# A hybrid attention layer on one core: a weight split sooner, a root's steps on another engine, and more banks for turns

## The chip, the core and the metric

The kernel runs on one core of a Trainium2 chip. Its engines are TensorE (PE, with PEld for its weight loads), VectorE (DVE), ScalarE (ACT), GpSimd (POOL) and SyncE (SP, which only issues transfers). The metric is the device time of one execution in microseconds; the time before is the median of three runs.

## The reference

One decoder layer over 2048 tokens of width 1024. The input is normalised and modulated, and one projection feeds two mixers: forgetting attention over 8 heads (causal, with a cumulative log gate) and sliding-window attention over 8 query heads with 2 key/value heads, window 128 and sinks. Each result is multiplied by a SiLU gate path, both are joined, projected, normalised and added to the input.

```python
mod = jax.nn.silu(c) @ w_ada[l] + b_ada[l]
shift, scale, gate = jnp.split(mod, 3, axis=-1)
h = rms_norm(x, g_pre[l]) * (1.0 + scale[:, None, :]) + shift[:, None, :]
proj = h @ w_in[l]
qa, ka, va, fa, za, qb, kb, vb, zb = jnp.split(proj, split_points, axis=-1)
oa = forgetting_attention(..., fa + b_fgate[l]) * jax.nn.silu(za)
ob = sliding_window_sink_attention(rope(qb), rope(kb), vb, sinks[l]) * jax.nn.silu(zb)
y = jnp.concatenate([oa, ob], axis=-1) @ w_out[l]
x = x + gate[:, None, :] * rms_norm(y, g_post[l])
```

## The kernel before

**Numbers and shapes.** Each float32 operand is held as two float16 parts, high and low, and each product is three matmuls: high by high, high by low, low by high. The tokens are taken in four groups of 512 (`ci`, 0 to 3). The normalised, modulated input of a group is `hT[ci]`, transposed: 8 tiles `k` of 128 features by 512 tokens, each with a high and a low part.

**From x to hT.** For each group, `load_x` brings four tiles `xt` of 128 tokens; `squares` (L404, ScalarE) sums their squares; `root` takes the reciprocal root by an integer seed (L100, L105, L106), a halving (L107) and three Newton steps (L114, L115, L117), all on VectorE; `normal` (L416, VectorE; L414, ScalarE, in group 0) scales the tiles. `turn(ci, k)` transposes one feature tile on TensorE into one of five banks of the pool `ps_x` (L422); its `scaled` applies the factors `Gp` and `Shp` on ScalarE (L428: one pass for even `k` to the high part, and one to `hf`; for odd `k` only `hf`), and its `split` makes the high part of odd `k` (L432) and all low parts (L433) on VectorE.

**The opening.** The modulation is computed from `w_ada`; then a maximum over the bound of h goes through two tiny matmuls (L641, L644) and gives `Gp` and `Shp`. Turns 0 to 4 of group 0 are done before that, the last three follow as banks come free, and the steps of `root(1)` are threaded between the splits of group 0.

**Weights.** A 128-column block of the input weights is a key: kb, vb, zb0 to zb3, qb0 to qb3, va, qk, za. Each is loaded (`w_load`, GpSimd's queue, L216, 512 KB), its maximum taken on VectorE (`w_max`, L222) and sent to memory and back to all partitions (`w_back`, L225 and L230), turned into a scale (`w_scale`), and split into a high part on ScalarE (`w_high`, L256) and a low one on VectorE (`w_low`, L262).

**The order.** All unit lists are concatenated by `add` into `punits`. A unit is the work of one `k` for kb, zb and qb (three matmuls, L339), or of half a token tile for vb (twelve, L777); eight units make one chunk of 512 tokens, after which the bank is evacuated in steps that `after` puts a number of ticks later. `events` holds the small steps by the number of the unit in front of which they are issued: `at_slice` adds one, and `add` sets a key's preparation by its lead ahead of the key's first unit. Within a region each engine issues in the order written. A group of tokens is kb, vb, zb0 (24 units), and the 8 turns of the next group are strewn among them after the units in `at_` (32 entries a group); group 3 has kb and vb alone. Then come qb0, zb0, qb0, zb1 up to unit `N_PRO` = 144. From there on 32 windows of the sliding-window attention (`Pair`: scores, maxima, exps, turn, pv) share TensorE with the remaining units up to `N_SWA`, spread evenly: 296 units. Forgetting attention and the output projection follow.

The rotary step of kb and qb chunks (`evac_rope`) copies the projection (L731), swaps halves by four transfers `qs` on SP's queue (L733), multiplies by the cosine (L736) and sine (L746), and adds (L747). `spread` brings the tables for a group.

Of the kernel before, what the change touches and what calls it, by code (L numbers as in the profile page):

```python
# [10 lines left out]
F32 = mybir.dt.float32  # L11
# [8 lines left out]
P = 128  # L20
# [23 lines left out]
def hybrid_layer(  # L44
# [46 lines left out]

    def rsqrt_mean(dst, ss, n):

        for _ in rsqrt_parts(dst, ss, n):
            pass

    def rsqrt_parts(dst, ss, n, more=None):
        v = sm(n, "rs_v")
        if more is None:
            V.tensor_scalar(v[:], ss, 1.0 / D, EPS, op0=ALU.mult, op1=ALU.add)  # L100
        else:
            V.scalar_tensor_tensor(v[:], ss, 1.0 / D, more, op0=ALU.mult, op1=ALU.add)
        y = sm(n, "rs_y")
        h = small.tile([P, n], I32, tag="rs_h", name="rs_h")
        V.tensor_scalar(h[:], v[:].bitcast(I32), 1, None, op0=ALU.logical_shift_right)  # L105
        V.tensor_scalar(y[:].bitcast(I32), h[:], -1, 0x5F3759DF, op0=ALU.mult, op1=ALU.add)  # L106
        V.tensor_scalar(v[:], v[:], -0.5, None, op0=ALU.mult)  # L107
        for it in range(3):
            yield
            t = sm(n, "rs_t")  # L110
            if n == 1:
                V.scalar_tensor_tensor(t[:], y[:], y[:], v[:], op0=ALU.mult, op1=ALU.mult)
            else:
                V.tensor_tensor(t[:], y[:], y[:], op=ALU.mult)  # L114
                V.tensor_tensor(t[:], t[:], v[:], op=ALU.mult)  # L115
            y2 = dst if it == 2 else sm(n, "rs_y")
            V.scalar_tensor_tensor(y2[:], t[:], 1.5, y[:], op0=ALU.add, op1=ALU.mult)  # L117
            y = y2
# [287 lines left out]
    def root(ci):  # L406
        ss, rst = rstd[ci]
        rsqrt_mean(rst, ss[:], 4)

# [7 lines left out]

    def turn(ci, k):

        px = ps_x.tile([P, CH], F32, tag="x", name="px")  # L420
        for u in range(4):
            PE.transpose(px[:, u * P:(u + 1) * P], xt[ci * 4 + u][:, k * P:(k + 1) * P], ident[:])  # L422
        hf = hst.tile([P, CH], F32, tag="hf", name="hf")
        hi, lo = hT[ci][:, 0, k, :], hT[ci][:, 1, k, :]

        def scaled():
            for dst in ([hi] if k % 2 == 0 else []) + [hf[:]]:
                A.activation(dst, px[:], AF.Identity, scale=Gp[:, k:k + 1], bias=Shp[:, k:k + 1])  # L428

        def split():  # L430
            if k % 2:
                V.tensor_copy(hi, hf[:])  # L432
            V.tensor_tensor(lo, hf[:], hi, op=ALU.subtract)  # L433

        return scaled, split
# [17 lines left out]
    with tc.manual_schedule():  # L453
# [186 lines left out]

        PE.transpose(bk[0][0:1, 0:P], bmx[:], ident[:])  # L641
        bm = st.tile([1, 1], F32, name="bm")
        V.tensor_reduce(bm[:], bk[0][0:1, 0:P], axis=AX.X, op=ALU.max)
# [6 lines left out]

        V.tensor_scalar(pfl[:], ipH[:], 0.5, None, op0=ALU.mult)
        root1 = rsqrt_parts(rstd[1][1], rstd[1][0][:], 4)
        for k in range(KT):
            turned[k][0]()
            turned[k][1]()
            if k >= 2:
                next(root1, None)
            if k + 5 < KT:
                turned.append(turn(0, k + 5))
        V.tensor_reduce(mxs[:, 2:3], wq["zb0"][0][:], axis=AX.XY, op=ALU.max, apply_absolute_value=True)  # L660
# [279 lines left out]
    def add(key, us):  # L940
        if key not in pkeys and key not in ("kb", "vb"):
            at = len(punits) - {"za3": 4}.get(key, 20 if key[:2] == "za" else 0)
            for n, (lead, f) in enumerate(((42, lambda: w_load(key, pieces(key))), (31, lambda: w_max(key)),
# [3 lines left out]
                if n >= 4 and key[:2] in ("qk", "za"):  # L947
                    lead -= 1
                if n < 4 and key in ("qb0", "zb1"):
                    lead += (16, 14, 12, 4)[n]  # L950
                if key == "zb0":
                    if n >= 3:
                        events.setdefault((13, 13, 14, 15, 16)[n - 3], []).append(f)
                else:
                    events.setdefault(max(at - lead, n), []).append(f)
# [30 lines left out]
    for ci in range(NCH):  # L986
# [3 lines left out]
        if ci < 3:  # L990
            add(*others[ci])

            mine, punits[n0:] = punits[n0:], []
            at_ = ([14, 16, 17, 18, 19, 20, 21, 22], [6, 8, 10, 12, 14, 16, 18, 20], [6, 7, 9, 10, 12, 13, 15, 16])[ci]
            for n, u in enumerate(mine):
# [3 lines left out]
            if ci < 2:  # L999

                for u in range(4):
                    at_slice(n0 + (3 if ci else 9) + u, lambda ci=ci, u=u: squares(ci + 2, (u,)))
                    at_slice(len(punits) - (0 if ci else 10) + u, lambda ci=ci, u=u: normal(ci + 2, (u,)))
                at_slice(len(punits) - 13, lambda ci=ci: root(ci + 2))
            at_slice(n0 + 12, lambda ci=ci: spread(ci + 1))
# [5 lines left out]
    add("qb0", qb_units(0, 1))  # L1011
    add(*others[4])
    N_PRO = len(punits)
    for n in range(4):
        at_slice(N_PRO + 20 + 3 * n, lambda: next(fx["sums"], None))
    qbs = [(f"qb{c_ // 4}", qb_units(c_ // 4, c_ % 4)) for c_ in range(2, 16)]
    n_o = 5
    for n, (key, us) in enumerate(qbs):
        add(key, us)
        lim = 5 + 5 * (n + 1) // 4 if n + 1 < len(qbs) else len(others)  # L1020
        for key2, us2 in others[n_o:lim]:
            add(key2, us2)
        n_o = lim
# [705 lines left out]
```

## Time and profile before

| What | Value |
|---|---|
| Median of three runs | 1177.23 us (1176.5 to 1177.47) |
| Profiled execution, its own time | 1173.47 us |
| Its span | 1171.7 us |
| TensorE busy | 1126.7 us (96%) |
| VectorE busy | 924.3 us (79%) |
| ScalarE busy | 661.7 us (56%) |
| GpSimd busy | 182.4 us (16%) |
| Chain that ended last, by engine | PE 74%, DVE 13%, DMA 7%, ACT 3%, issue 2% |

Busy time is the union of an engine's instructions. TensorE's includes matmuls stretched by a lower granted clock. The chain is followed back from the last instruction, at each step to what released it. In a timeline row the columns are start, duration, engine, line, operation and tiles, and in brackets the idle time before it with what ended that.

### The profile page before, as it was taken

The page shows a single profiled execution, that of the slowest core. Times are in us where ns is not written, and L with a number is a line of the kernel's source. Part 1 is how long each engine was busy: PE and PEld are TensorE (multiplying, and loading weights), DVE is VectorE, ACT ScalarE, POOL GpSimd, SP SyncE. Part 2 cuts the span into 40 slices and gives each one's busy share as a digit, 9 for nine tenths or more (in the row PEclk, how much of TensorE's full clock was granted, in tenths as well). Part 3 has the DMA queues.
Part 4 walks back from the last instruction along what each step waited for, and adds up shares of the span by engine and source line. Part 5 has one row for each costly group of instructions (what it writes and reads, how often), then busy time and mean ns, then how long its engine had stood idle before and what let it go on. Part 6 is the DMA issues. An engine that isn't in the chain of part 4 may idle for free.

```text
span 1171.7 us, 26770 instructions
## 1 busy us (share of the span) xinstructions
PE 1126.7 (96%) x10637; PEld 671.1 (57%) x10637; DVE 924.3 (79%) x2167; ACT 661.7 (56%) x1150; POOL 182.4 (16%) x293
## 2 busy tenths in 40 slices
PE   5899999999999999999999999999999999999997
PEld 2476555765558876555555555555556555544444
DVE  7876668677776548788888999888897897778885
ACT  2784445454555421476666767666676788633332
POOL 1000125535454421010000100001000000000000
PEclk9899999999999999999999999999999999999999
DMA  9745333314324323423424332222311237677742
GB/s 333 259 142 88 82 94 78 91 52 108 95 70 95 48 60 74 67 56 86 74 71 65 106 55 58 61 49 67 52 37 43 72 88 226 138 216 200 193 144 108
DMA packets 123481, 120.19 MB, mean 103 GB/s; under 512 B 64948, under 2 KB 100828, under 8 KB 123356
## 3 DMA queue, kind: packets, MB, share of 16 engines
q1 hardware_dynamic: 112088, 85.69, 27.1%
q0 software_dynamic: 10832, 32.50, 13.0%
q8 instruction: 83, 1.36, 0.6%
q14 instruction: 42, 0.34, 0.2%
q10 hardware_dynamic: 436, 0.28, 0.1%
HBM read 64.75 MB, written 25.18 MB: 77 GB/s over the span
## 4 chain that ended last, share of the span: by engine, by line
PE 74%; DVE 13%; DMA 7%; ACT 3%; issue 2%; SPq 1%; POOL 0%; DVEq 0%; ACTq 0%; POOLq 0%
PE bk L339 27%; PE bk L1522 13%; PE bk L357 7%; PE sta L1311 4%; PE sta L1310 4%; PE bk L1261 4%; PE poa L1336 3%; PE poa L1337 3%; PE poa L1334 3%; DMA wa<-in_w_ada_dram 2%; DVE a_m L1264 2%; PE pss L871 1%; PE pob L924 1%; DVE pha L1324 1%; PE pxb L900 1%
## 5 line engine op out<-in xcount | busy, mean ns | idle before, releaser
L1317 ACT ACTIVATE p<-sta,lift,scl_qk 128x1024 f32<-128x1024 f32 (+2 forms) x160 | 171.9, 1075 | 131.1 <-PE sta L1311 80.4
L339 PE MATMUL bk<-hT,wh_qk 128*128 128x512 f16 x768 | 194.7, 378 | 0.0
L1324 DVE TENSOR_TENSOR pha<-p,pha 128x1024 f16<-128x1024 f32 (+2 forms) x160 | 169.1, 1057 | 0.2 <-ACT pha L1321 0.2
L1264 DVE TENSOR_REDUCE a_m<-bk 128x1 f32<-128x512 f32 x192 | 130.4, 686 | 46.5 <-PE bk L1261 45.5
L1522 PE MATMUL bk<-wohl,oz 128*128 128x512 f16 x744 | 165.3, 379 | 1.0 <-DVE oz L1471 0.7
L1321 ACT ACTIVATE pha<-p 128x1024 f16<-128x1024 f32 (+2 forms) x160 | 148.1, 925 | 7.1 <-PE bk L1261 2.3
L1522 PEld LDWEIGHTS <-oz 128*128 128x128 f16 x744 | 71.9, 99 | 82.8 <-DVE oz L1471 1.8
L1337 PE MATMUL poa<-vt,pha 128*128 128x65 f16 x1088 | 116.0, 192 | 1.4 <-DVE pha L1324 1.4
L1334 PE MATMUL poa<-vt,pha 128*128 128x65 f16 x1088 | 116.6, 193 | 0.8 <-DVE ona L1343 0.7
L1336 PE MATMUL poa<-vt,pha 128*128 128x64 f16 x1088 | 116.6, 194 | 0.0
L339 PEld LDWEIGHTS <-wh_qk 128*128 128x128 f16 x768 | 72.2, 97 | 74.4 <-issue 1.9
L1310 PE MATMUL sta<-T 128*128 128x512 f16 (+1 forms) x320 | 110.9, 346 | 2.8 <-ACT p L1317 2.8
L1261 PE MATMUL bk<-T 66*128 66x512 f16 (+2 forms) x320 | 109.7, 348 | 2.5 <-DVE a_m L1264 1.9
L1334 PEld LDWEIGHTS <-pha 128*128 128x128 f16 x1088 | 101.5, 96 | 15.5 <-DVE ona L1343 1.9
L1311 PE MATMUL sta<-T 69*128 69x512 f16 (+1 forms) x320 | 109.8, 348 | 0.0
L1336 PEld LDWEIGHTS <-pha 128*128 128x128 f16 x1088 | 100.9, 97 | 11.4
L1337 PEld LDWEIGHTS <-pha 128*128 128x128 f16 x1088 | 100.8, 99 | 1.8 <-DVE pha L1324 1.8
L339 PE MATMUL bk<-hT,wh_za 128*128 128x512 f16 x384 | 99.7, 378 | 0.0
L357 PE MATMUL bk<-wh_va,hT 128*128 128x128 f16 x1536 | 91.9, 221 | 2.9 <-issue 2.8
L357 PEld LDWEIGHTS <-hT 128*128 128x128 f16 x1536 | 88.7, 99 | 7.4 <-issue 5.4
L339 PE MATMUL bk<-hT,wh_zb 128*128 128x512 f16 x384 | 88.9, 379 | 0.0
L339 PE MATMUL bk<-hT,wh_qb 128*128 128x512 f16 x384 | 87.6, 379 | 0.7 <-DVE wh_qb L262 0.7
(447 smaller groups left out, 1893.1 us busy)
## 6 DMA issues: line engine op xcount, KB each, us to landing
hT<-in_x_dram SPq DMA_DIRECT2D x20, 512.0 KB
wa<-in_w_ada_dram SPq DMA_DIRECT2D x16, 512.0 KB
z_d<-tz POOLq DMA_DIRECT2D x32, 256.0 KB
T<-stq SPq DMA_DIRECT2D x64, 128.0 KB
T<-z_d SPq DMA_DIRECT2D x16, 512.0 KB
out_dram<-hT SPq DMA_DIRECT2D x15, 512.0 KB
xt<-in_x_dram SPq DMA_DIRECT2D x12, 512.0 KB
qs<-qf SPq DMA_DIRECT2D x80, 64.0 KB
```

What stands on the lines that cost most here:

```text
L339: PE.matmul(ps, whl[:, a, k, :], hT[ci][:, b, k, :], start=(k == 0 and n == 0), stop=(k == KT - 1 and n == 2))
L357: PE.matmul(ps[:, u * P:(u + 1) * P], hT[ci][:, a, k, u * P:(u + 1) * P], whl[:, b, k, :], start=(k == 0 and n == 0), stop=(k == KT - 1 an ...
L1261: PE.matmul(mx[:, :w], T[0:XM, 0, i * P:(i + 1) * P], T[0:XM, 2, pc * CH:pc * CH + w], start=True, stop=True)
L1264: V.tensor_reduce(m3[:, u, pc:pc + 1], mx[:, :w], axis=AX.X, op=ALU.max)
L1310: PE.matmul(self.st[:, o:o + w], T[:, 3, kb_], T[:, 1, qc], start=True, stop=False)
L1311: PE.matmul(self.st[:, o:o + w], T[0:XR, 2, kb_], T[0:XR, 0, qc], start=False, stop=not diag)
L1317: A.activation(self.p32[:, :self.w], self.st[:, :self.w], AF.Exp, scale=scl[f"qk{self.hd}"][:], bias=lift[:])
L1324: V.tensor_tensor(self.ph[:, 1, :self.w], self.p32[:, :self.w], self.ph[:, 0, :self.w], op=ALU.subtract)
L1334: PE.matmul(po[:, u, :], ph[:, 0, pq], vt[:, b, hd, 0:65], start=(self.first and n == 0 and u == 0), stop=False)
L1336: PE.matmul(po[:, u, 0:64], ph[:, 0, pq], vt[:, b, hd, 65:VW], start=False, stop=False)
L1337: PE.matmul(po[:, u, :], ph[:, 1, pq], vt[:, b, hd, 0:65], start=False, stop=(self.last and n == len(self.blocks) - 1))
L1522: PE.matmul(py, self.hl[:, i, k, :], w_slot(8 * j + k)[:, cc], start=(k == 0 and m_ == 0), stop=(k == KT - 1 and m_ == 2))
```

## The change

1. `root(ci)` for the groups 1 to 3 does the halving and the Newton steps on GpSimd; the seed stays on VectorE. GpSimd takes two operations where VectorE has one fused, so a root has 13 operations there.
2. Turns 5 and 6 of group 0 go into the banks `bk[1]` and `bk[2]`, issued between the two tiny matmuls; turn 7 is issued behind the scaling of turn 0. `root(1)` is issued as a whole ahead of the scalings.
3. zb1 is loaded at unit 6, its maximum taken at 38, sent back at 46, scaled at 67, split at 71 to 75. Its chunks 0 and 1 become units of the third token group (ci = 2), which then has 40 units, and chunk 2 takes the place that chunk 0 had. `N_PRO` becomes 160, and the windows hold 280 units.
4. The turns of group 3 are strewn after the units 14, 16, ... 28 of that group instead of 6, 7, ... 16.
5. Places of the small steps: `root(2)` at unit 14 instead of 19; `squares(3)` at 56 to 59 instead of 35 to 38; `root(3)` at 61 instead of 51; `normal(3)` at 68 to 71 instead of 64 to 67.
6. In the windows, the order of the other keys' chunks is adapted: one of zb1's chunks is left for the first three qb chunks.

```diff
@@ -89,12 +89,13 @@
         V.tensor_scalar(t[:], src, 1.0e-30, None, op0=ALU.max)
         V.tensor_scalar(dst.bitcast(I32), t[:].bitcast(I32), 0x7F800000, None, op0=ALU.bitwise_and)
 
-    def rsqrt_mean(dst, ss, n):
-
-        for _ in rsqrt_parts(dst, ss, n):
+    def rsqrt_mean(dst, ss, n, eng=None):
+
+        for _ in rsqrt_parts(dst, ss, n, eng=eng):
             pass
 
-    def rsqrt_parts(dst, ss, n, more=None):
+    def rsqrt_parts(dst, ss, n, more=None, eng=None):
+        W = eng or V
         v = sm(n, "rs_v")
         if more is None:
             V.tensor_scalar(v[:], ss, 1.0 / D, EPS, op0=ALU.mult, op1=ALU.add)
@@ -104,17 +105,21 @@
         h = small.tile([P, n], I32, tag="rs_h", name="rs_h")
         V.tensor_scalar(h[:], v[:].bitcast(I32), 1, None, op0=ALU.logical_shift_right)
         V.tensor_scalar(y[:].bitcast(I32), h[:], -1, 0x5F3759DF, op0=ALU.mult, op1=ALU.add)
-        V.tensor_scalar(v[:], v[:], -0.5, None, op0=ALU.mult)
+        W.tensor_scalar(v[:], v[:], -0.5, None, op0=ALU.mult)
         for it in range(3):
             yield
             t = sm(n, "rs_t")
             if n == 1:
-                V.scalar_tensor_tensor(t[:], y[:], y[:], v[:], op0=ALU.mult, op1=ALU.mult)
+                W.scalar_tensor_tensor(t[:], y[:], y[:], v[:], op0=ALU.mult, op1=ALU.mult)
             else:
-                V.tensor_tensor(t[:], y[:], y[:], op=ALU.mult)
-                V.tensor_tensor(t[:], t[:], v[:], op=ALU.mult)
+                W.tensor_tensor(t[:], y[:], y[:], op=ALU.mult)
+                W.tensor_tensor(t[:], t[:], v[:], op=ALU.mult)
             y2 = dst if it == 2 else sm(n, "rs_y")
-            V.scalar_tensor_tensor(y2[:], t[:], 1.5, y[:], op0=ALU.add, op1=ALU.mult)
+            if eng is None:
+                V.scalar_tensor_tensor(y2[:], t[:], 1.5, y[:], op0=ALU.add, op1=ALU.mult)
+            else:
+                W.tensor_scalar(t[:], t[:], 1.5, None, op0=ALU.add)
+                W.tensor_tensor(y2[:], t[:], y[:], op=ALU.mult)
             y = y2
 
     def root_scale(dst, ss):
@@ -405,7 +410,7 @@
 
     def root(ci):
         ss, rst = rstd[ci]
-        rsqrt_mean(rst, ss[:], 4)
+        rsqrt_mean(rst, ss[:], 4, G if ci else None)
 
     def normal(ci, us=range(4)):
         for u in us:
@@ -415,9 +420,9 @@
             else:
                 V.tensor_scalar(xt[t], xt[t], r, None, op0=ALU.mult)
 
-    def turn(ci, k):
-
-        px = ps_x.tile([P, CH], F32, tag="x", name="px")
+    def turn(ci, k, px=None):
+
+        px = px or ps_x.tile([P, CH], F32, tag="x", name="px")
         for u in range(4):
             PE.transpose(px[:, u * P:(u + 1) * P], xt[ci * 4 + u][:, k * P:(k + 1) * P], ident[:])
         hf = hst.tile([P, CH], F32, tag="hf", name="hf")
@@ -639,6 +644,7 @@
         V.tensor_reduce(bmx[:], bnd[:], axis=AX.X, op=ALU.max)
 
         PE.transpose(bk[0][0:1, 0:P], bmx[:], ident[:])
+        turned += [turn(0, k, bk[k - 4]) for k in (5, 6)]
         bm = st.tile([1, 1], F32, name="bm")
         V.tensor_reduce(bm[:], bk[0][0:1, 0:P], axis=AX.X, op=ALU.max)
         PE.matmul(bk[0][:, P:P + 1], ones[0:1, :], bm[:], start=True, stop=True)
@@ -649,14 +655,12 @@
         V.tensor_scalar(Shp[:], shf[:], ipH[:], 2.0 ** 14, op0=ALU.mult, op1=ALU.mult)
 
         V.tensor_scalar(pfl[:], ipH[:], 0.5, None, op0=ALU.mult)
-        root1 = rsqrt_parts(rstd[1][1], rstd[1][0][:], 4)
+        root(1)
         for k in range(KT):
             turned[k][0]()
             turned[k][1]()
-            if k >= 2:
-                next(root1, None)
-            if k + 5 < KT:
-                turned.append(turn(0, k + 5))
+            if k == 0:
+                turned.append(turn(0, 7))
         V.tensor_reduce(mxs[:, 2:3], wq["zb0"][0][:], axis=AX.XY, op=ALU.max, apply_absolute_value=True)
         for key in ("kb", "vb"):
             kaps[key] = kappa(pws[key], key)
@@ -946,8 +950,10 @@
                                            (5, lambda: w_low(key, 1)), (4, lambda: w_done(key)))):
                 if n >= 4 and key[:2] in ("qk", "za"):
                     lead -= 1
-                if n < 4 and key in ("qb0", "zb1"):
+                if n < 4 and key == "qb0":
                     lead += (16, 14, 12, 4)[n]
+                if key == "zb1":
+                    lead = at - (6, 38, 46, 67, 71, 73, 75, 77)[n]
                 if key == "zb0":
                     if n >= 3:
                         events.setdefault((13, 13, 14, 15, 16)[n - 3], []).append(f)
@@ -989,9 +995,12 @@
         add("vb", vb_units(ci))
         if ci < 3:
             add(*others[ci])
+            if ci == 2:
+                add(*others[4])
+                add(*others[5])
 
             mine, punits[n0:] = punits[n0:], []
-            at_ = ([14, 16, 17, 18, 19, 20, 21, 22], [6, 8, 10, 12, 14, 16, 18, 20], [6, 7, 9, 10, 12, 13, 15, 16])[ci]
+            at_ = ([14, 16, 17, 18, 19, 20, 21, 22], [6, 8, 10, 12, 14, 16, 18, 20], [14, 16, 18, 20, 22, 24, 26, 28])[ci]
             for n, u in enumerate(mine):
                 punits.append(u)
                 if n in at_:
@@ -999,9 +1008,9 @@
             if ci < 2:
 
                 for u in range(4):
-                    at_slice(n0 + (3 if ci else 9) + u, lambda ci=ci, u=u: squares(ci + 2, (u,)))
-                    at_slice(len(punits) - (0 if ci else 10) + u, lambda ci=ci, u=u: normal(ci + 2, (u,)))
-                at_slice(len(punits) - 13, lambda ci=ci: root(ci + 2))
+                    at_slice(n0 + (24 if ci else 9) + u, lambda ci=ci, u=u: squares(ci + 2, (u,)))
+                    at_slice(len(punits) + (4 if ci else -10) + u, lambda ci=ci, u=u: normal(ci + 2, (u,)))
+                at_slice(len(punits) - (3 if ci else 18), lambda ci=ci: root(ci + 2))
             at_slice(n0 + 12, lambda ci=ci: spread(ci + 1))
     n0 = len(punits)
     at_slice(n0, lambda: open_fox())
@@ -1009,15 +1018,15 @@
     add("qb0", qb_units(0, 0))
     add(*others[3])
     add("qb0", qb_units(0, 1))
-    add(*others[4])
+    add(*others[6])
     N_PRO = len(punits)
     for n in range(4):
         at_slice(N_PRO + 20 + 3 * n, lambda: next(fx["sums"], None))
     qbs = [(f"qb{c_ // 4}", qb_units(c_ // 4, c_ % 4)) for c_ in range(2, 16)]
-    n_o = 5
+    n_o = 7
     for n, (key, us) in enumerate(qbs):
         add(key, us)
-        lim = 5 + 5 * (n + 1) // 4 if n + 1 < len(qbs) else len(others)
+        lim = (7, 8, 8)[n] if n < 3 else 5 + 5 * (n + 1) // 4 if n + 1 < len(qbs) else len(others)
         for key2, us2 in others[n_o:lim]:
             add(key2, us2)
         n_o = lim
```

## The prediction

> **What bounds the kernel now.** I read the page first (span and busy lines), then the busy time of each engine in stretches through the opening projections, then the timelines of TensorE, ScalarE, VectorE and the queues there, and last the waits of the sliding-window stage.
>
> ```profile
> span 1171.7 us, 26770 instructions
> ## 1 busy us (share of the span) xinstructions
> PE 1126.7 (96%) x10637; PEld 671.1 (57%) x10637; DVE 924.3 (79%) x2167; ACT 661.7 (56%) x1150; POOL 182.4 (16%) x293
> ```
>
> TensorE is the bound, 96% busy. The change adds and removes no matmul, so it can only move the end by the time that TensorE loses in the stretch that it reorders. That stretch, cut at the borders of its unit groups (columns as in the first line, each engine's busy time with its instructions):
>
> ```profile
> core 0: us, PE busy (x) PEld busy (x) DVE busy (x) ACT busy (x) POOL busy (x), PEclk, DMA share, GB/s
> 46.14:56.32 10.18, 8.84 (x36) 4.60 (x36) 8.93 (x26) 7.32 (x11) 0.00 (x0) 0.83 0.45 144
> 56.32:72.42 16.10, 15.32 (x157) 12.10 (x156) 14.43 (x46) 12.07 (x22) 0.00 (x0) 1.00 0.66 221
> 72.42:79.61 7.19, 6.09 (x29) 2.80 (x28) 6.85 (x13) 6.00 (x9) 0.00 (x0) 1.00 0.31 74
> 79.61:93.55 13.94, 13.94 (x150) 11.15 (x149) 8.13 (x27) 10.66 (x21) 1.47 (x2) 1.00 0.44 110
> 98.25:117.68 19.43, 17.18 (x156) 12.92 (x157) 10.07 (x18) 7.73 (x14) 2.56 (x4) 0.91 0.68 87
> 117.68:129.88 12.20, 11.18 (x121) 8.02 (x120) 10.69 (x29) 5.29 (x9) 1.09 (x2) 1.00 0.48 102
> ```
>
> "Busy" also counts matmuls drawn out by a slow clock, so I set the stretches against clean rates. The chain that ended last has undisturbed runs of both matmul shapes:
>
> ```profile
> 124.37 5.68 PE bk L777 x96
> ...
> 158.50 5.93 PE bk L339 x27
> ```
>
> 96 vb matmuls take 5.68 us (0.71 a unit of 12), and one 512-wide matmul 0.22 (0.66 a unit of 3, 5.27 for 24). The stretch from 79.61 to 93.55 has no idle time: 5.68 + 5.27 leaves 2.99 for its seven turns, 0.43 each. Then the third group's stretch (one kb unit, 8 vb, 8 zb0, 8 turns) should take 0.66 + 5.68 + 5.27 + 3.44 = 15.05 and takes 19.43: 4.4 lost. The fourth group's kb and vb should take 10.95 and take 12.20: 1.25 lost. The first kb chunk with three turns should take 6.56 and takes 10.18: 3.6 lost. The two stretches from 56.32 to 79.61 lose 1.2 and 1.5, with 0.5 allowed for the small matmuls of the zb0 maximum. So about 12 us are there to be won, 1% of the span.
>
> **The change part by part.**
>
> *Turns into two more banks, the first root's Newton steps off VectorE.* TensorE:
>
> ```profile
> 43.86 0.38 PE L644 MATMUL bk<-bm,ones 1*128 1x1 f32 x2 [0.37 <-DVE bm L643]
> ```
>
> The eight transposes of turns 5 and 6 now stand just ahead of L644: 0.87 us from about 43.4, so L644 starts near 44.3, and Gp, on which all scaling waits, is 0.45 late. That is a cost on the path. ScalarE behind it:
>
> ```profile
> 45.31 0.78 ACT L428 ACTIVATE hT<-px,Shp,Gp 128x512 f16<-128x512 f32 x1 [2.76 <-DVE pfl L651]
> ...
> 51.96 1.50 ACT L428 ACTIVATE hf<-px,Shp,Gp 128x512 f32<-128x512 f32 x2
> ```
>
> It needs the same 8.1 us for its 12 scalings (45.31 to 53.46) and ends at 53.9. VectorE ended its splits here:
>
> ```profile
> 55.15 0.69 DVE L433 TENSOR_TENSOR hT<-hf,hT 128x512 f16<-128x512 f32 x1
> ```
>
> A cast and a subtraction, about 1.0 us, have to follow the last scaling: 54.9 instead of 55.84, because ten small Newton operations left this loop, which had drawn it 1.4 us past what ScalarE's end requires. The seed's three operations come before the loop, while VectorE waits for the first scaling anyway. Gain 0.9. This root's result is wanted only by a normalisation some 10 us later.
>
> *The second root, and what the transfers allow (to the end of the second kb chunk).*
>
> ```profile
> 65.21 0.16 DVE L100 TENSOR_SCALAR rs_v<-ss 128x4 f32<-128x4 f32 x1
> ...
> 67.40 0.16 DVE L117 SCALAR_TENSOR_TENSOR rst<-rs_t,rs_y 128x4 f32<-128x4 f32 x1
> 67.80 0.69 DVE L746 TENSOR_TENSOR qs<-qs,sinT 128x512 f32<-128x512 f32 x1 [0.24 <-DMA qs<-qf]
> ...
> 70.74 1.41 DVE L416 TENSOR_SCALAR xt<-xt,rst 128x1024 f32<-128x1024 f32 x2
> ...
> 78.38 0.69 DVE L433 TENSOR_TENSOR hT<-hf,hT 128x512 f16<-128x512 f32 x1
> ```
>
> 13 operations run from 65.21 to 67.56, 0.18 each; ten leave, 1.8 us, ahead of the splits that hold up the second kb chunk until 79.07. With the 0.9 that would be 2.7. But L746 was waiting for its transfer qs, so qs decides what is kept, and qs is queued behind the loads of x:
>
> ```profile
> 50.41 4.84 SPq L397 DMA_DIRECT2D xt<-in_x_dram  x8
> ```
>
> The loads wait for the last turn of group 0, which now needs only the first turn's bank: two scalings from 45.8 end at 47.1, the turn at 47.6, 2.8 sooner than 50.4. Against that zb1's 512 KB join them. I allow 1.3 us, from the 403 GB/s of this stretch:
>
> ```profile
> 30.00:40.00 10.00, 9.54 (x16) 4.12 (x17) 7.65 (x21) 9.07 (x12) 0.00 (x0) 0.69 1.02 403
> ```
>
> qs comes 1.5 sooner. I take **1.5** (bounds 0 and 2.7) by the end of the second kb chunk.
>
> *The third root, its squares, and the third group.* VectorE, and TensorE's wait for it:
>
> ```profile
> 85.23 0.69 DVE L433 TENSOR_TENSOR hT<-hf,hT 128x512 f16<-128x512 f32 x1 [5.23 <-ACT hf L428]
> ```
>
> ```profile
> PE px L422 <- DVE xt L416: 2.3, 4, 0.9
> ```
>
> ```profile
> 97.60:101.10 3.50, 1.60 (x6) 0.51 (x4) 3.50 (x6) 0.00 (x0) 0.56 (x1) 1.00 0.43 100
> 101.10:104.50 3.40, 3.05 (x14) 2.18 (x15) 2.47 (x4) 2.34 (x4) 1.45 (x2) 0.50 0.23 82
> 104.50:108.00 3.50, 3.50 (x55) 3.48 (x53) 1.63 (x4) 2.13 (x4) 0.00 (x0) 1.00 1.45 40
> ```
>
> The squares of the last token group stood on ScalarE ahead of the third group's scalings and left VectorE idle 5.23 us; VectorE then reached the last normalisations far behind TensorE, whose turns waited 2.3 us for them, and after 3.5 us with 1.60 busy the granted clock was 0.50 for 3.4 us. That makes up the 4.4. Now these squares go behind the third group's turns, and the fourth's turns start eight units later in their group. Does the normalisation make it?
>
> ```profile
> L404 ACT ACTIVATE junk<-xt x8: 1047/1056/1059, 57.0 to 82.7; 128x1024 bf16<-128x1024 f32 x8
> L404 ACT ACTIVATION_READ_ACCUMULATOR junk<-xt x8: 185/187/201, 58.0 to 83.7; 128x1 f32 x8
> ```
>
> Before the squares' place (unit 56) TensorE has 8 vb, 2 zb0 and 5 turns from 79.61 on, 9.15 us: 87.3 with the 1.5. Four squares (5.0) and one turn's scalings (1.3) end at 93.6, the seed at 94.2. TensorE reaches the turn at 98.25 - 1.5 + 0.66 + 7 x 0.71 = 102.4, and four normalisations take 2.7. So GpSimd has 5.5 us for 13 operations, 0.42 each. No row shows such operations on it; the nearest are these:
>
> ```profile
> L910 POOL TENSOR_SCALAR_AFFINE_SELECT ptb<-fold 128x512 f16<-128x512 f16 x64 | 40.7, 636 | 54.2 <-ACT fold L905 51.3 <-DVE fold L906 2.7
> ...
> L1713 POOL MEMSET const-float32-0.0<- 128x1 f32 x1 | 0.1, 99 | 0.3 <-issue 0.3
> ```
>
> 0.10 to 0.64 each; four elements are nearest to the memset of one, and each step waits for the one before: I take 0.25, 3.3 us for a root. That fits by 2.2 us here, and by 1.0 at the second root, where 4.3 pass between the seed's end (64.9) and the first normalisation (69.2 for 70.74). So the 4.4 return whole.
>
> The page "TensorE: Matmul & The Clock Gate" of the Trainium skill (Part 1) says that the clock halves after a whole idle window of about 3.4 us. By that rule none of these waits would have cost clock, the 2.1 us beyond the 2.3 of waiting would stay lost, and the forecast would be 1174.2. The trace disagrees: the longest of the four waits was 0.9 us, and the clock fell. I keep the rows.
>
> *Two chunks of zb1 in the third group.* 16 units, 10.5 us of TensorE work, move ahead of the fourth kb chunk. Its splits have that much longer, so the 1.25 lost there return. zb1's load goes past GpSimd's z_d store and qb0's load; its maximum and split on VectorE come where that engine idled. Behind its round trip through memory GpSimd holds a z_d store, qb0's load and, 15 units on, the third root; none is wanted within 7 us. For small stalls around the moved pieces (bounds 0 and 2.3, one more wait like L416's) I charge 0.8.
>
> *The sliding-window stage gives them up.* Its 32 windows held 296 units, now 280: 0.33 us less cover in each.
>
> ```profile
> ACT fold L905 <- PE pxb L900: 31.5, 25, 3.8
> ```
>
> In 25 of them ScalarE waited for TensorE's transposes, so that cover isn't missed. In seven it may be: at most 2.3. I take 1.2.
>
> **Sum.** 1.5 + 4.4 + 1.25 - 0.8 - 1.2 = 5.15 us sooner. The profiled execution took 1173.47 (1.8 beside the span): 1168.3. The median of the runs is 3.8 higher, 1177.23, and I keep that distance: **1172.1**.
>
> **The rivals.**
> - *Newton on GpSimd is slow, and it ends slower.* At 0.64 us an operation a root takes 8.3. The second root holds VectorE's normalisation up 4.0, the third the turns 2.8, and that gap halves the clock again, about 2: 5.15 - 8.8 = 3.65 slower, 1180.9. It crosses zero near 0.50 an operation. For it: GpSimd's long row is 0.64. Against: that row has 128 times the elements. The page "GPSIMD Engine Reference" of the Trainium skill (section 4.1) advises VectorE for elementwise work, GpSimd being about twice as slow with two inputs; no run here shows it yet. By it, an estimate of 0.36 us from VectorE's 0.18, a root takes 4.7 and is 0.4 late once: 1172.5.
> - *zb1's load runs badly beside x.* Between 104.50 and 108.00, above, the DMA engines were full at only 40 GB/s. Should that happen for 8 us from 48 on, x and qs come 5.2 late, the squares and the zb0 split behind them hold TensorE, and the gap halves the clock: 5.15 - 1.5 - 5.2 - 2 = 3.55 slower, 1180.8. Against it: one such stretch, and an empty queue before the x loads into which zb1 may slip.
> - *The windows give it all back.* If each window is as long as its chain of scores, maxima and exponentials, 10.5 us are lost: 4.15 slower, 1181.4. The 25 waits speak against it.
>
> **How the numbers follow.** Forecast 0.65, with an own range of 1168.9 (2.7 + 4.4 + 1.25 kept, nothing lost) to 1174.7 (half of it spoilt); slow GpSimd 0.13, bad load 0.12, windows 0.10. 0.2% is 2.4 us, about what can be told from no change. The rivals act by degrees: a fifth of their 0.35 still ends faster, two fifths the same. Faster 0.72, same 0.14, slower 0.14. The range is 1168.5 to 1178.5; only the rivals at their full prices lie outside.
>
> **What would show it.** No TensorE wait for L416 at the fourth group's turns, and a full clock there; the last squares behind the third group's turns on ScalarE; GpSimd's 13 operations a root at about 0.25 us; the x loads near 47.6; the first L746 near 66.3; no new TensorE waits in the windows. I am wrong if GpSimd's operations exceed 0.42, if zb1's load delays x, or if TensorE idles over 2 us more in the windows.

## The result, and the profile after

Medians: 1175.43 us after (14 runs, 1172.07 to 1180.7), 1176.55 before (14 runs, 1173.54 to 1179.46); ratio 0.9993, 95% interval 0.9979 to 1.0006. That is no change that this measurement can tell; 1.1 us sooner at best guess, where 5.15 was forecast. The profiled execution after took 1175.42 us.

```profile
span 1173.7 us, 26784 instructions
...
PE 1129.2 (96%) x10637; PEld 671.6 (57%) x10637; DVE 920.0 (78%) x2137; ACT 661.1 (56%) x1150; POOL 196.6 (17%) x332
```

Busy time of the engines of the changed kernel, in stretches cut at the borders that the prediction used: both kb chunks to the end of the second; the second group's rest; the third group, which now holds 16 units more; the fourth group's kb and vb.

```profile
core 0: us, PE busy (x) PEld busy (x) DVE busy (x) ACT busy (x) POOL busy (x), PEclk, DMA share, GB/s
46.22:77.88 31.66, 29.27 (x212) 18.26 (x212) 27.51 (x60) 25.37 (x41) 9.12 (x24) 0.95 0.57 176
77.88:91.81 13.93, 13.93 (x150) 11.15 (x149) 8.72 (x19) 7.76 (x16) 1.70 (x3) 1.00 0.34 82
91.81:126.29 34.48, 32.01 (x226) 20.38 (x225) 22.86 (x48) 19.52 (x34) 7.22 (x19) 0.95 0.40 92
126.29:137.15 10.86, 10.86 (x122) 8.03 (x121) 4.84 (x17) 2.76 (x5) 1.44 (x2) 1.00 0.38 104
```

Before, the same stretches took 33.47, 13.94, 24.13 and 12.20 (from its borders 46.14, 79.61, 93.55, 117.68, 129.88). With 10.54 for the 16 moved units (5.27 for eight, as in the prediction), the third group takes 23.94: 0.2 of its 4.4 has come back. The first stretch gained 1.8 and the fourth 1.3. From there to the end of the span it is 1036.55 after, and 1041.82 - 10.54 = 1031.28 before: 5.3 later. The profiled execution before lies 3.1 us below the median of its kernel (1173.47 against 1176.55), the one after at its median, so part of these 5.3 can be the difference between two executions.

The third group first, in the timeline of the changed kernel (start, duration, engine and line, and in brackets the idle time before it and what ended that):

```profile
79.39 2.47 SPq L737 DMA_DIRECT2D qs<-qf  x4
79.69 0.54 POOL L230 DMA_DIRECT2D mx_d<-w_mx  x1 [0.50 <-DVE w_mx L227]
...
88.62 0.54 POOL L235 DMA_DIRECT2D mxr<-mx_d  x1 [8.39 <-DMA mx_d<-w_mx]
...
89.09 0.69 DVE L750 TENSOR_TENSOR qs<-qs,sinT 128x512 f32<-128x512 f32 x1 [4.18 <-DMA cosT<-cs__234]
...
90.54 0.63 ACT L754 ACTIVATE stb<-qc 128x512 f16<-128x512 f32 x1 [3.95 <-DVE qc L751]
...
97.64 0.17 DVE L101 TENSOR_SCALAR rs_v<-ss 128x4 f32<-128x4 f32 x1 [1.53 <-ACT junk L409]
...
98.78 0.38 PE L344 MATMUL bk<-hT,wh_kb 128*128 128x512 f16 x1 [2.03 <-DVE hT L437]
```

The four qs transfers were issued by 81.9, and VectorE could use them at 89.1. (The bracket of L750 names cosT because its signal came last; that transfer stands behind qs on the same queue and brings a table for the next group, which L750 does not read.) ScalarE, which issues in order, stood 3.95 us before `stb`, its float16 copy of the rotated chunk. The moved squares behind it came that much later: the third root's seed, forecast at 94.2, started at 97.64. The last scalings and splits stood behind the squares, and TensorE waited. Its granted clock then fell to 0.52 (in the columns of the stretches above). On the chain that ended last the 84 vb matmuls behind that wait take 6.60 us, where the rate of the 96 in 5.68 gives 4.97.

```profile
100.50:103.90 3.40, 3.40 (x35) 3.40 (x33) 1.92 (x6) 1.63 (x2) 2.64 (x9) 0.52 0.03 11
```

```profile
100.10 6.60 PE bk L781 x84
```

Then the first windows, in the columns of a timeline:

```profile
153.25 0.54 POOL L230 DMA_DIRECT2D mx_d<-w_mx  x1 [3.29 <-DVE w_mx L227]
153.51 2.41 SPq L737 DMA_DIRECT2D qs<-qf  x4
...
167.88 0.69 DVE L750 TENSOR_TENSOR qs<-qs,sinT 128x512 f32<-128x512 f32 x1 [6.25 <-DMA qs<-qf]
...
169.33 0.63 ACT L754 ACTIVATE stb<-qc 128x512 f16<-128x512 f32 x1 [8.42 <-DVE qc L751]
...
171.01 0.63 POOL L914 TENSOR_SCALAR_AFFINE_SELECT ptb<-fold 128x512 f16<-128x512 f16 x1 [7.55 <-ACT fold L909]
...
172.29 0.23 PE L928 MATMUL pob<-vb,ptb 128*128 128x64 f16 x2 [1.24 <-POOL ptb L916]
```

Again qs is late (12.0 us from the end of its issues to its use), ScalarE's stb with it, behind stb the `fold` (the transposed exponentials copied to float16), behind that GpSimd's masking (`ptb`), and TensorE at the end. Both times a `mx_d` write, the 512 bytes of a weight's maxima as 128 pieces of four bytes, was issued within 0.3 us of the first qs transfer. In the kernel before, the zb1 maximum stood elsewhere, and qb1's write went out 2.2 us ahead of a qs that VectorE came to 13 us later, at 171.3, and found there. This became the theory: such a write holds, for 8 to 9 us, whatever is issued beside or just behind it, on any queue. It is put to the test from *max_third* on; the expectations of the first four runs were written ahead of it and name other theories.

### The profile page after: what moved, and what is told of

It reads as the page before. It is cut to its first block, busy times and chain, and to the rows that moved or that the text cites. A ratio compares the mean times of both kernels' runs of the same rounds, so it can differ in the third digit from the quotient of the medians.

```text
span 1173.7 us, 26784 instructions
## 1 busy us (share of the span) xinstructions
PE 1129.2 (96%) x10637; PEld 671.6 (57%) x10637; DVE 920.0 (78%) x2137; ACT 661.1 (56%) x1150; POOL 196.6 (17%) x332
## 4 chain that ended last, share of the span: by engine, by line
PE 73%; DVE 13%; DMA 6%; ACT 3%; issue 2%; SPq 1%; POOL 1%; ACTq 0%; DVEq 0%
PE bk L344 27%; PE bk L1531 13%; PE bk L362 5%; PE sta L1320 4%; PE sta L1319 4%; PE bk L1270 4%; PE poa L1345 3%; PE poa L1346 3%; PE poa L1343 3%; DMA wa<-in_w_ada_dram 2%; DVE a_m L1273 2%; DVE pha L1333 1%; PE pob L928 1%; PE pss L875 1%; PE bk L781 1%
## 5 line engine op out<-in xcount | busy, mean ns | idle before, releaser
L1326 ACT ACTIVATE p<-sta,lift,scl_qk 128x1024 f32<-128x1024 f32 (+2 forms) x160 | 171.8, 1074 | 130.9 <-PE sta L1320 81.9
```

Of the source, the lines that this page charges most:

```text
L1326: A.activation(self.p32[:, :self.w], self.st[:, :self.w], AF.Exp, scale=scl[f"qk{self.hd}"][:], bias=lift[:])
```

## The experiments

All times are medians; ratios are to the kernel before, with 95% intervals. The edits are shown in excerpts.

### The changed kernel again, and its parts

*again* has no edit.

> The changed kernel once more, unaltered, for a second profile of it. Theory (chance): in the first profile the third kb chunk's qs took over 8 us to land because one slow transfer held it, so ScalarE wrote stb late, the moved squares came in front of the last two turns' scalings, and TensorE lost 2.0 + 0.35 + 1.65 us near 98 to 106; likewise wr_va's slow load held the first window's qs for 12.5 us. If that is chance, the second profile has qs landing within 4 us there, no TensorE wait for the last hT split, and qb0's first matmul about 6 us sooner than in the kernel before instead of 3.1. Rival (order): the squares' place makes it, whatever qs does; then the seed's wait for the squares (1.5 us) and TensorE's wait of about 2 us are there again. Median time, by either: 0.5 to 2 us below the kernel before.

1175.12 us (12 runs; before 1176.37, 35 runs; 0.9990, 0.9975 to 1.0004). In its profile everything stands where it stood:

```profile
89.39 0.69 DVE L750 TENSOR_TENSOR qs<-qs,sinT 128x512 f32<-128x512 f32 x1 [4.71 <-DMA sinT<-sp__232]
```

TensorE's wait of 2.03 us is there again, at 99.09. So it is no chance; the windows' waits recur as well. Whether the squares' place makes the wait by itself, this run's rival, stays open up to *third_far*. Only the size in the windows varies: the rest of the span from qb0 on is here 3.1 us longer than before, where the first profile had 5.3.

*third_only* has neither the extra banks nor GpSimd's steps:

```diff
-        rsqrt_mean(rst, ss[:], 4, G if ci else None)
+        rsqrt_mean(rst, ss[:], 4)
-        turned += [turn(0, k, bk[k - 4]) for k in (5, 6)]
-        root(1)
+        root1 = rsqrt_parts(rstd[1][1], rstd[1][0][:], 4)   # stepped in the loop, as before
```

> Only the third part: two zb1 chunks behind the third token group with zb1's earlier load and split, the squares and root of the last group behind the third group's turns, the fourth group's turns later. The turns of group 0 stay in two banks and all Newton steps on VectorE. Theory (the windows and the third group give back what they gain): 0 to 1.5 us below the kernel before; the first two stretches as before (first L750 near 67 to 68, second kb chunk's end near 79.6), the 1.25 us of the fourth group's kb and vb gained, and 2 to 5 us more of TensorE's idle time between 150 and 200 us. Rival (GpSimd is the culprit): without GpSimd's steps this part brings its whole 5 us less the 1.7 of the front: 3 us or more below the kernel before.

1178.02 us (1.0009, 0.9994 to 1.0024): 1.6 us above the kernel before, which the interval does not tell from no change. It lies above the theory's range and contradicts the rival: without GpSimd's steps the moved units bring nothing.

*front_only* puts the third group, zb1's places and the windows back as before:

```diff
-            if ci == 2:
-                add(*others[4])
-                add(*others[5])
-                    at_slice(n0 + (24 if ci else 9) + u, ... squares(ci + 2, (u,)))
+                    at_slice(n0 + (3 if ci else 9) + u, ... squares(ci + 2, (u,)))
```

> Only the first two parts: turns 5 and 6 of group 0 in two more banks, and the Newton steps of three roots on GpSimd; zb1 stays in the windows and the last squares stay in front of the third group's scalings. Theory: the front's 1.2 us by the first kb chunk and 1.7 by the second are there and nothing later gives them back but the third group's normalisations, which wait for GpSimd: 1 to 2 us below the kernel before. Rival (GpSimd is the culprit): its operations take 0.3 to 0.46 us on the mean, the third root ends 2 us later than on VectorE, the third group's turns wait longer than their 2.3 us, and the time is equal to the kernel before or up to 2 us above.

1174.49 us (0.9991, 0.9976 to 1.0006): 1.9 us below, as the theory said, though the interval includes no change. The way there is another than the theory's: the stretch up to the second chunk's end is 2.2 us shorter, the third group takes 2.9 less, and the fourth kb and vb then give back 4. Here qb0's write, issued 0.1 us behind the first qs, holds that qs.

```profile
114.94 0.69 DVE L750 TENSOR_TENSOR qs<-qs,sinT 128x512 f32<-128x512 f32 x1 [8.50 <-DMA cosT<-cs__234]
```

*vec_newton* undoes GpSimd's steps alone (the lines on `root` in third_only's edit).

> The changed kernel with the Newton steps of all roots on VectorE, the first of them stepped inside the scaling loop as in the kernel before. Theory: VectorE's 30 small steps (5.4 us) come back ahead of its splits; 0 to 1 us above the changed kernel. Rival (GpSimd is the culprit): its roots of 5.3, 6.0 and 4.3 us and VectorE's waits of 0.7 and 1.4 us for them go, and the time is 1.5 us or more below the changed kernel.

1179.67 us (1.0022, 1.0009 to 1.0036): 4.5 us above the changed kernel (1175.12 in *again*). Both sides missed it, the rival by far: GpSimd's steps pay. The last root's 13 operations stand on VectorE ahead of the split that TensorE waits for, and the wait of 2.03 us there becomes 3.62:

```profile
102.81 1.74 PE L344 MATMUL bk<-hT,wh_kb 128*128 128x512 f16 x3 [3.62 <-DVE hT L437]
```

### Moving the writes

```diff
-                    lead = at - (6, 38, 46, 67, 71, 73, 75, 77)[n]
+                    lead = at - (6, 43, 56, 67, 71, 73, 75, 77)[n]   # max_third, max_both
+                    lead = at - (6, 50, 62, 67, 71, 73, 75, 77)[n]   # third_far
+                if key == "qb1" and n in (1, 2):                     # max_window, max_both
+                    lead -= 5
```

> The changed kernel with the maximum of zb1, and so its 512-byte write mx_d of 128 four-byte pieces, five units later (and its return ten units later), behind the third chunk's qs instead of beside it. Theory (the write holds what is issued beside and behind it for 8 to 9 us): qs lands within 4 us of its last issue, VectorE's wait of 4.2 us at L750 goes, the last squares run some 4 us sooner, TensorE's waits of 2.0 and 0.35 us and the half clock behind them go, and qb0 starts near 133.5 instead of 137.2 to 137.5; the windows lose as much as before, so the whole is about 3.5 us below the changed kernel. Rival (the squares' place, or the spread transfers on the same queue, hold ScalarE): qs is as late, and the time is that of the changed kernel within 1 us.

1177.48 us (1.0001, 0.9982 to 1.0021): the forecast gain of 3.5 us did not come. The run does not decide about the theory, since VectorE, ahead of TensorE here, came to the maximum almost at once. The write still went out among the four qs transfers, which were issued from 78.57 to 81.05, and VectorE waited longer than in the changed kernel:

```profile
80.21 0.75 POOL L230 DMA_DIRECT2D mx_d<-w_mx  x1 [1.85 <-DVE w_mx L227]
...
90.69 0.69 DVE L750 TENSOR_TENSOR qs<-qs,sinT 128x512 f32<-128x512 f32 x1 [6.59 <-DMA cosT<-cs__234]
```

> The changed kernel with the maximum of qb1 and its return five units later, behind the qs of qb0's second chunk (now mx_d is issued 0.3 us ahead of it, at 153.3). Theory (the write holds what stands beside it): that qs lands within 5 us of issue instead of 12.5, the waits of TensorE for ptb (1.9 to 2.2 us) and for wh_va (1.6 us) and the half clock at 173 to 182 go, and the windows' first hundred microseconds lose 5 us less: about 5 us below the changed kernel, unless the write now holds another transfer. Rival (lost cover: 280 units instead of 296 in the windows): the same waits stay wherever the write stands, and the time is that of the changed kernel within 1 us.

1177.25 us (0.9996, 0.9985 to 1.0008). The forecast gain of 5 us did not come, but the profile shows where it went:

```profile
160.82 0.54 POOL L230 DMA_DIRECT2D mx_d<-w_mx  x1 [9.82 <-DVE w_mx L227]
161.68 0.92 POOL L221 DMA_DIRECT2D wr_va<-in_w_in_dram  x1 [0.32 <-ACT sm__1886 L897]
...
162.59 0.69 DVE L750 TENSOR_TENSOR qs<-qs,sinT 128x512 f32<-128x512 f32 x1
...
175.19 1.22 DVE L227 TENSOR_REDUCE w_mx<-wr_va 128x1 f32<-128x1024 f32 x1 [6.47 <-DMA wr_va<-in_w_in_dram]
```

With the write behind it, qs was there without a wait. Now the load of wr_va, 0.9 us behind the write, was held, VectorE stood 6.47 us for it, and TensorE waited for the cosine step behind that. From the waits of TensorE between 125 and 250 us (in total, times, longest):

```profile
PE bk L344 <- DVE qc L740: 4.4, 1, 4.4
```

The rival foretold the old waits, for ptb and wh_va; these are gone.

> Both moves of the writes together. Theory: the two gains add, about 8 us below the changed kernel and 9 below the kernel before (near 1167). Rival (squares' place and lost cover): no change against the changed kernel.

1178.35 us (1.0008, 0.9993 to 1.0022): neither move helped by itself, and both together did not, where the theory forecast 8 us.

> The changed kernel with zb1's maximum and write (128 pieces) twelve units later and its return sixteen, so that VectorE comes to it some 5 us or more behind qs; five units later had moved the write by only 1 us. Theory: qs lands within 4 us of its last issue, the last squares run 4 us sooner, TensorE's waits of 2.0 and 0.35 us near 97 to 100 and the half clock behind them go, and qb0 starts near 133.5; the windows lose as before, the whole 2 to 4 us below the changed kernel. Rival (squares' place): the same 2 us wait, time as the changed kernel within 1 us.

1178.3 us (1.0005, 0.9993 to 1.0017): again no gain, where 2 to 4 us were forecast. In the third group the theory's mechanism holds against the rival: with the squares where the changed kernel has them, the write goes out behind qs, stb is written 4 us sooner than in the changed kernel (90.54), and TensorE's waits for the splits are gone. But the return, sixteen units later, now stands behind the last root on GpSimd, and VectorE waits for it ahead of the normalisations:

```profile
84.44 0.54 POOL L230 DMA_DIRECT2D mx_d<-w_mx  x1 [6.04 <-DVE w_mx L227]
...
86.56 0.63 ACT L754 ACTIVATE stb<-qc 128x512 f16<-128x512 f32 x1 [0.76 <-DVE qc L751]
...
98.45 0.60 POOL L235 DMA_DIRECT2D mxr<-mx_d  x1
...
101.88 0.29 DVE L246 TENSOR_REDUCE w_mx<-mxr 128x1 f32<-128x128 f32 x1 [5.80 <-DMA mxr<-mx_d]
...
103.73 1.05 PE L427 MATMUL px<-ident,xt 128*128 128x128 f32 x2 [2.40 <-DVE xt L421]
```

The stall only moved on.

### Adding a write, and changing its form

*write_added*: the kernel before, and one such write more, beside the qs of the second kb chunk. Nothing reads it.

```diff
                 A.activation(qf[:], ps, AF.Copy, scale=PS_SCALE)
+                if pool and ci == 1:
+                    G.dma_start(mx_e[:], qf[:, 0:1])
```

> The kernel before with one write more: when the second kb chunk's qf is ready, GpSimd writes one column of it (128 pieces of four bytes) to memory beside the four qs transfers; nothing reads it. Theory (such a write holds what stands beside it): qs, which in the kernel before is there when VectorE comes to L746 at 92.2, lands 8 to 9 us after 85.7, VectorE waits 2 us or more there, and the third group's turns and their clock lose 2 to 4 us: slower than the kernel before by 1 to 4 us. Rival (512 bytes cost nothing): no wait at L746, and the time of the kernel before within 0.5 us.

1179.81 us (1.0023, 1.0009 to 1.0037): 2.4 us slower for 512 bytes, as the theory said. In the profiled execution, its slowest, the mechanism is plain:

```profile
85.35 2.48 SPq L736 DMA_DIRECT2D qs<-qf  x4
85.62 0.54 POOL L734 DMA_DIRECT2D mx_e<-qf  x1 [5.12 <-ACT qf L732]
...
98.98 0.69 DVE L749 TENSOR_TENSOR qs<-qs,sinT 128x512 f32<-128x512 f32 x1 [7.06 <-DMA cosT<-cs__235]
...
101.05 1.01 PE L340 MATMUL bk<-hT,wh_kb 128*128 128x512 f16 x2 [4.90 <-DVE hT L434]
```

*rows_write* and *rows_before* turn every such write, in the kernel after and before, from 128 pieces of 4 bytes into 4 pieces of 128:

```diff
-        V.tensor_reduce(mx[:], wq[key][0][:], ...)
+        V.tensor_reduce(mx[:, 0:1], wq[key][0][:], ...)    # mx: a zeroed 128x32 tile
-        G.dma_start(md[:], mx[:])
+        V.transpose(mt[:], mx[:])                          # by 32x32 blocks
+        G.dma_start(md.rearrange("(b c) o -> b (c o)", b=4),
+                    mt[:].rearrange("(b r) c -> b r c", b=4)[:, 0, :])
```

> The changed kernel with every mx_d write made of 4 pieces of 128 bytes instead of 128 pieces of 4: the maxima stand in one column of a 128x32 tile, VectorE transposes its 32x32 blocks (one operation more, some 0.2 us), and the four rows that hold them are written. Theory (the 128 small pieces hold the transfer engines for 8 to 9 us, and all that is issued beside or behind them): the write is back within 3 us, the third chunk's qs and the first window's qs land within 4 us, wr_va is not slow, TensorE's waits near 97 to 107 and 170 to 200 go, and the whole is 6 to 10 us below the changed kernel (about 1167). Rival (any write and read back takes that long, or the squares' place and the lost cover make the waits): the same waits at the same places and a time within 1 us of the changed kernel.

> The kernel before with the same 4-piece writes. Theory: here only some of the writes stand beside a transfer that is waited for (zb1's load at 102.8 to 112, the loads at 128, 392 and 483), so it gains less than the changed kernel does: 1 to 4 us below the kernel before, and the changed kernel with such writes is then 3 us or more below this one. Rival (lost cover): both gain alike, and the changed kernel keeps its 1 us over the kernel before or loses it.

rows_write: 1160.01 us, ratio 0.9854 (0.9841 to 0.9867). rows_before: 1166.56 us, ratio 0.9914 (0.9898 to 0.9929). Both beat both kernels, and between them the change now brings 6.5 us. Both gained more than the theory forecast (6 to 10 us, and 1 to 4): from qb0 to the end alone 9.5 us of the kernel after and 5.3 of the kernel before went with the old form. The transfers' issues by group (count, KB each, median us from issue to landing), in the changed kernel and in rows_write:

```profile
mx_d<-w_mx POOLq DMA_DIRECT2D x23, 0.5 KB, 7.9
```

```profile
mx_d<-w_mt POOLq DMA_DIRECT2D x23, 0.5 KB, 1.7
```

In rows_write the write goes out where it did in the changed kernel, among the qs transfers of the third chunk, and nothing waits for them any more. So it is in the first window, where the first qs is issued at 149.01:

```profile
79.47 2.47 SPq L743 DMA_DIRECT2D qs<-qf  x4
80.01 0.61 POOL L236 DMA_DIRECT2D mx_d<-w_mt  x1 [0.76 <-DVE w_mt L235]
...
84.91 0.68 DVE L756 TENSOR_TENSOR qs<-qs,sinT 128x512 f32<-128x512 f32 x1
...
149.00 0.59 POOL L236 DMA_DIRECT2D mx_d<-w_mt  x1 [3.53 <-DVE w_mt L235]
...
157.05 0.68 DVE L756 TENSOR_TENSOR qs<-qs,sinT 128x512 f32<-128x512 f32 x1
```

The stretches of rows_write, at the same borders:

```profile
46.67:77.96 31.29, 29.16 (x212) 18.27 (x212) 27.48 (x60) 25.40 (x41) 8.74 (x24) 0.95 0.57 180
77.96:91.89 13.93, 13.93 (x150) 11.15 (x149) 10.82 (x23) 11.68 (x22) 1.82 (x3) 1.00 0.47 115
91.89:121.78 29.89, 29.89 (x225) 18.79 (x224) 21.99 (x51) 15.51 (x27) 7.37 (x19) 1.00 0.37 93
121.78:132.65 10.87, 10.87 (x122) 8.04 (x121) 4.02 (x12) 2.77 (x5) 1.46 (x2) 1.00 0.37 98
```

and of rows_before:

```profile
45.49:78.83 33.34, 31.25 (x220) 20.09 (x220) 30.19 (x83) 25.40 (x41) 0.00 (x0) 0.91 0.51 168
78.83:92.76 13.93, 13.93 (x150) 11.15 (x149) 8.11 (x27) 10.65 (x21) 1.46 (x2) 1.00 0.44 108
92.76:115.41 22.65, 20.39 (x177) 13.94 (x176) 19.66 (x39) 14.14 (x24) 2.63 (x4) 1.00 0.41 104
115.41:126.27 10.86, 10.86 (x121) 8.03 (x120) 6.05 (x21) 2.77 (x5) 1.68 (x3) 1.00 0.46 98
```

In rows_write TensorE is busy without a gap from 77.96 to 132.65, at the full clock. The third group takes 29.89 - 10.54 = 19.35 against 22.65. Without the old writes the kernel before loses nothing in its fourth group either.

*rows_vec* is rows_write with all Newton steps on VectorE.

> The changed kernel with the 4-piece writes and all Newton steps on VectorE, for the price of the GpSimd steps where no write holds a transfer. Theory (the steps cost by whose queue they stand in: on VectorE they stand ahead of the splits that TensorE waits for): the first kb chunk's matmuls end 1.1 us later, the second's 0.6, and the last split of the third chunk 2.3 us later with a wait of TensorE of about 1 us and a slower clock behind it: 2 to 4 us above the changed kernel with 4-piece writes. Rival (GpSimd's steps of 0.2 to 0.65 us cost as much as VectorE gains, since VectorE waits 0.7 and 1.4 us for them): within 1 us of it.

1163.57 us (0.9897, 0.9881 to 0.9913): 3.6 us above rows_write, as the theory said. TensorE waits 5.2 us between 44 and 125 us for scalings and splits (hT, hf), in rows_write 3.5. The stretch up to the second chunk's end takes 33.14 us against 31.29, the third group 30.38 against 29.89.

## Why the prediction was right in its range and wrong in its case

The time fell within the range, but in the case "same" (0.14), not in the forecast "faster" (0.72). Step by step:

- *First chunk and second chunk: right.* The x loads were issued at 47.40 (47.6 forecast), the splits of the first chunk ended at 54.71 (54.9), L650, the old L644, held VectorE for 0.90 us instead of 0.47 (0.45 forecast as its delay), and the second chunk's end gained 1.8 (1.5). zb1's load went out at 37.58, 9.8 us ahead of the x loads instead of beside them, so the second rival did not come about in the form given.
- *GpSimd's steps: mis-sized, without harm to the sign.* I took 0.25 us an operation. In the changed kernel's groups by line (count, busy us, mean ns):

```profile
L121 POOL TENSOR_SCALAR rs_t<-rs_t 128x4 f32<-128x4 f32 x9 | 3.7, 412 | 0.8
L115 POOL TENSOR_TENSOR rs_t<-rs_y 128x4 f32<-128x4 f32 x9 | 3.4, 380 | 0.5
L116 POOL TENSOR_TENSOR rs_t<-rs_t,rs_v 128x4 f32<-128x4 f32 x9 | 3.4, 375 | 0.7
```

  The three roots took 5.3, 6.0 and 4.3 us instead of 3.3, and VectorE waited 0.7 and 1.4 us for the second and third. That this still costs TensorE less than the same steps on VectorE, vec_newton and rows_vec show. With the shorter operations of L108 and L122 the mean over all 39 is 0.33 us. That lies near the estimate of 0.36 which the prediction worked out from "GPSIMD Engine Reference" (section 4.1) of the Trainium skill. The advice there to keep such work on VectorE would have cost 3.6 us here (rows_vec against rows_write); that the steps' place ahead of the splits in VectorE's order makes the difference is read from vec_newton's row.
- *Third group, 4.4 "return whole": the step that failed.* The waits for L416, now L421, did go. But I let squares, seed and turns follow from ScalarE's durations, with ScalarE at work without a stop, and never asked when stb, which stands ahead of the squares, would get its qs. zb1's write had been moved beside that qs. I had counted its return as something that holds up nothing, and its landing time I had not priced. Only 0.2 of the 4.4 came back. With the write in 4 pieces the seed starts at 93.66, close to the forecast 94.2, and the group takes 19.35 us, 4.8 less than before; 1.5 of these come to the kernel before as well by the new form alone (22.65).
- *Fourth group, 1.25: right in size, wrong in cause.* It came (1.3), but that the splits had longer was not needed for it. In the kernel before, qs of that stretch was late by qb0's write at 102.81, and VectorE waited 5.89 us for it at L746; rows_before loses nothing there, without any move.
- *The windows, 1.2: right in size without the old writes, not in cause.* From qb0 on rows_write takes 1159.7 - 132.65 = 1027.05 and rows_before 1162.8 - 126.27 - 10.54 = 1025.99: 1.1 us more. TensorE's waits do not show cover missing in seven windows: there is one wait for a split of va's weights, 1.4 us long, which rows_before lacks. Why that split is late was not followed.

```profile
PE bk L368 <- DVE wh_va L273: 1.4, 1, 1.4
```

  The other 2 to 4 us in the changed kernel, and the waits for ptb, went with the old form of the writes; qb1's had come to stand beside a qs by the shift of 16 units.
- *The stretch from 104.50 to 108.00*, which the prediction showed with full DMA engines at 40 GB/s, was the clue. I put it to the load of zb1 and made it a rival; it was the write 0.56 us ahead of that load. With its form changed, in rows_before, the DMA engines move 172 GB/s from 103 to 107 us, where they take up that load and qs.
- *The sum.* With writes that hold nothing, the change brings 6.5 us by medians, and 4.3 by these two profiles from the first kb unit on (2.05 + 3.30 - 1.06; the profile of rows_before is its fastest run, that of rows_write its slowest). Forecast were 5.15. That the measured time lay within the range is luck: the range was made wide for three other rivals, and the write beside qs, which took the gain away, was priced in none of its terms.

The longest wait ahead of the slow vb matmuls was 2.03 us, and the granted clock behind it 0.52. The rule of "TensorE: Matmul & The Clock Gate" (Part 1) of the Trainium skill, that the clock halves after a whole idle window of about 3.4 us, does not account for that: here too the trace disagrees with it.

## What to carry to other kernels

When steps are moved, list every transfer they issue, the smallest too, and look at what else goes out beside it and behind it until it has landed; price it by its time to landing, not by its bytes. A full DMA share at a low rate in a profile is worth following back to the transfer that was issued first. Write a column of 128 values as a few rows, not as 128 pieces.

## What the runs showed of the hardware

- A write of 512 bytes in 128 pieces took 7.9 us to land (median of 23) and held transfers issued beside it, from its own engine and from another: from the end of the issues to the use it took qs 7.2 and 12.0 us, and a 512 KB load 12.6. In 4 pieces of 128 bytes it took 1.7, and all 23 writes in this form were worth 10 us to the kernel before and 15 to the kernel after. "DMA: Bandwidth & Descriptors" of the Trainium skill (section "Issuing engines are not separate DMA queues") says that all queues share the same 16 engines; the traces agree. Its limit of 512 bytes a piece for full rate ("Specifications") does not part the two forms, which both lie below it; whether the pieces' number or their size decides was not tried.
- GpSimd's operations on 128x4 elements take 0.20 to 0.23 us in the third root's later steps, and 0.48 and 0.65 at 98.31 and 98.86, while VectorE runs a cast (98.30) and a subtraction (98.77) of 128x512. That VectorE's work stretches them is only read from this; no run took it away.
